# Five no-ops in place of two ahead of the first load on SyncE, in a rotary-embedding kernel

## The chip, the cores and the metric

One core of one Trainium2 chip. Times are device microseconds (us) of one execution, medians over several runs. An "interval" is the 95% interval of a ratio of times.

## The reference

```python
def reference(x, cos, sin, num_heads):            # x: 16 x 512 x 1024 f32, 16 heads of 64
    x = x.reshape(batch, seq, num_heads, head_dim)
    x1, x2 = x[..., :half_dim], x[..., half_dim:]
    cos, sin = cos[None, :, None, :], sin[None, :, None, :]     # 512 x 32 each
    return np.concatenate([x1 * cos - x2 * sin, x1 * sin + x2 * cos], axis=-1)
```

The kernel reads 33.5 MB and writes 33.5 MB; the two tables are 64 KB each.

## The kernel before

Eight tiles of 4 MB (128 partitions x 8 rows of 1024 floats). SyncE (SPq in the profile) issues all loads and stores of x and out on one queue; ScalarE (ACTq) issues the two tables on another. The start (comments put in here, cuts marked `# ...`):

```python
    nc.scalar.dma_start(out=sin_sb, in_=sin_v)        # L91, ScalarE's queue
    nc.scalar.dma_start(out=cos_sb, in_=cos_v)        # L92
    for _ in range(2):
        nc.sync.nop(hint="pause")                     # the two no-ops
    load(0, 0, FIRST[0])                              # tile 0, rows 0 to 2: 1.5 MB, 12 KB per partition
    for lo, hi in zip(FIRST, FIRST[1:]):
        load(0, lo, hi)                               # tile 0, rows 3 to 7: 20 KB per partition
    load(1)
    load(2)
    load_two(3)
    # ... identity matrix, then the tables are spread over 128 partitions by matmuls:
    nc.tensor.matmul(out=sin_t, lhsT=spread, rhs=sin_sb, start=True, stop=True)
    nc.tensor.matmul(out=cos_t, lhsT=spread, rhs=cos_sb, start=True, stop=True)
    # ... sns = (-sin, sin), in SBUF for GpSimd
```

Each tile: GpSimd multiplies by the sine rows (L175, `b`), DVE multiplies by the cosine (L151, into PSUM), multiplies one row of eight by the sine (L160) and adds most of the two (L199); PE and ScalarE add the rest. DVE starts when the cosine table is there, GpSimd when sine and the first x piece are. The kernel keeps five tiles in SBUF, so the later loads wait for stores:

```python
    def stores(t):
        if t == 4:
            store_two(3)
        elif t != 3:
            store(t)
        if t == 2:
            load(5)
            load_two(6)          # waits until the stores of tiles 1 and 2 have landed
```

## Time and profile before

| | before |
|---|---|
| time, median of 3 runs (spread) | 162.38 us (162.28 to 162.7) |
| span of the profiled run | 160.7 us |
| DVE, GpSimd busy | 136.3, 127.1 us |
| queue of x and out: share of 16 engines | 97.6% |
| sine, cosine landed | 7.2, 10.6 us |
| last store issued, landed | 148.23, 159.84 us |

A line of the timeline reads: start, duration, engine and line, operation, what it writes and reads, and in brackets how long the engine stood idle before and what ended that. From the timeline of the kernel before, the start of the two engines and the last store:

```profile
9.41 4.50 POOL L175 TENSOR_TENSOR b<-x,sns 128x2048 f32<-128x2048 f32 x1 [8.10 <-DVE sns L127]
...
12.18 1.23 DVE L151 TENSOR_TENSOR own_ps<-x,tab 128x1024 f32<-128x1024 f32 x1
...
148.23 0.33 SPq L83 DMA_DIRECT2D out_dram<-x  x1
```

GpSimd starts at 9.41 (released by the sine rows), DVE at 12.18 after the cosine table, and the last store is issued right after DVE's last sum; its 4 MB then take 11.6 us to land.

### The profile page before, as it was taken

What the parts mean: (1) busy time and instruction counts of PE and PEld (TensorE: products, weight loads), DVE (VectorE), ACT (ScalarE), POOL (GpSimd) and SP (SyncE); (2) the same over time, 40 slices, a digit from 0 to 9 for tenths busy, and PEclk for the clock granted to TensorE, in tenths of its full rate; (3) what the DMA queues carried; (4) which work ended last, traced back from release to release, by engine and by line L of the source; (5) the groups of instructions that cost most, each with busy time, mean ns of one, the idle gap of its engine ahead of it and who ended that gap; (6) DMA issues with size and microseconds to landing.
All of it is one profiled execution on the core that took longest, in us unless ns stands there. A gap on an engine that the chain in (4) does not pass through costs nothing.

```text
span 160.7 us, 433 instructions
## 1 busy us (share of the span) xinstructions
PE 57.2 (36%) x71; PEld 18.8 (12%) x71; DVE 136.3 (85%) x85; ACT 18.0 (11%) x25; POOL 127.1 (79%) x38
## 2 busy tenths in 40 slices
PE   3140825055503731191309250645047402922000
PEld 0110301021102210121003010211022101310000
DVE  1029999999999999999999999999999999998000
ACT  0000331003000301021100310031003010201000
POOL 1069999999999889988998899892999999960000
PEclk9999995558555765567555955585557655675555
DMA  5999999999999999999999999999999999999993
GB/s 168 411 431 458 408 473 424 392 449 465 392 449 449 408 392 506 408 392 498 410 400 465 441 400 441 465 392 432 473 400 416 489 400 416 473 408 408 392 506 147
DMA packets 2562, 67.25 MB, mean 419 GB/s; under 512 B 257, under 2 KB 385, under 8 KB 385
## 3 DMA queue, kind: packets, MB, share of 16 engines
q1 hardware_dynamic: 2400, 67.11, 97.6%
q10 hardware_dynamic: 160, 0.13, 0.2%
q14 instruction: 2, 0.01, 0.0%
HBM read 33.69 MB, written 33.55 MB: 418 GB/s over the span
## 4 chain that ended last, share of the span: by engine, by line
DVE 74%; issue 11%; DMA 6%; PE 1%; ACTq 0%; DVEq 0%
DVE x L199 34%; DVE pd L151 33%; DMA b<-in_cos_dram 6%; DVE pe_ps L151 5%; DVE own_ps L151 1%; PE tab L124 1%; ACTq L91 0%; DVE x L160 0%; DVE tab L129 0%; DVEq L199 0%
## 5 line engine op out<-in xcount | busy, mean ns | idle before, releaser
L175 POOL TENSOR_TENSOR b<-x,sns 128x2048 f32<-128x2048 f32 (+1 forms) x32 | 126.4, 3983 | 15.4 <-DVE sns L127 8.1
L199 DVE TENSOR_TENSOR x<-pd,b 128x2048 f32<-128x2048 f32 x24 | 54.9, 2288 | 0.9
L151 DVE TENSOR_TENSOR pd<-x,tab 128x2048 f32<-128x2048 f32 x24 | 55.0, 2292 | 0.2
L186 PE MATMUL own_ps<-x,ident 128*128 128x512 f32 x32 | 29.6, 1082 | 53.3 <-DVE x L160 48.3
L186 PE MATMUL pe_ps<-b,ident 128*128 128x512 f32 x32 | 25.1, 877 | 27.2 <-DVE pe_ps L151 27.2
L186 PEld LDWEIGHTS own_ps<-x,ident 128*128 128x128 f32 x32 | 9.4, 324 | 73.2 <-DVE x L160 59.3
L219 ACT COPY x<-own_ps 128x1024 f32<-128x1024 f32 x8 | 8.1, 1013 | 72.8 <-PE own_ps L186 72.8
L191 ACT COPY x<-pe_ps 128x512 f32<-128x512 f32 x16 | 9.4, 589 | 38.7 <-PE pe_ps L186 38.7
L186 PEld LDWEIGHTS pe_ps<-b,ident 128*128 128x128 f32 x32 | 8.2, 286 | 42.2 <-DVE pe_ps L151 33.9
L151 DVE TENSOR_TENSOR pe_ps<-x,tab 128x512 f32<-128x512 f32 x16 | 11.0, 687 | 0.0
L151 DVE TENSOR_TENSOR own_ps<-x,tab 128x1024 f32<-128x1024 f32 x8 | 9.8, 1224 | 0.0
L160 DVE TENSOR_TENSOR x<-x,tab 128x1024 f32<-128x1024 f32 x8 | 9.7, 1214 | 0.0
L126 DVE TENSOR_SCALAR sns<-pd 128x256 f32<-128x256 f32 x1 | 0.4, 425 | 7.0 <-PE pd L123 7.0
L219 ACT ACT_TABLE_LOAD x1 | 1.3, 1283 | 16.8 <-DVE x L160 16.8
L123 PE MATMUL pd<-b,spread 64*128 64x256 f32 x2 | 1.2, 696 | 4.7 <-DMA b<-in_sin_dram 4.7
L129 DVE COPY tab<-sns 128x64 f32<-128x64 f32 x1 | 0.2, 228 | 2.6 <-PE tab L124 2.6
L124 PE MATMUL tab<-b,spread 64*128 64x256 f32 x2 | 1.2, 708 | 2.1 <-DMA b<-in_cos_dram 2.1
L111 PE MATMUL own_ps<-zero 128*128 128x512 bf16 x2 | 1.0, 622 | 1.2 <-DVE zero L107 1.2
L123 PEld LDWEIGHTS pd<-b,spread 64*128 64x128 f32 x2 | 0.5, 306 | 5.6 <-issue 5.6
L107 DVE MEMSET zero<- 128x256 uint32 x1 | 0.3, 272 | 0.9 <-PEq L250 0.9
L124 PEld LDWEIGHTS tab<-b,spread 64*128 64x128 f32 x2 | 0.5, 310 | 2.9 <-DMA b<-in_cos_dram 2.9
L111 PE MATMUL pe_ps<-zero 128*128 128x512 bf16 x1 | 0.6, 634 | 0.0
(9 smaller groups left out, 1.8 us busy)
## 6 DMA issues: line engine op xcount, KB each, us to landing
out_dram<-x SPq DMA_DIRECT2D x6, 4096.0 KB, 21.4
x<-in_x_dram SPq DMA_DIRECT2D x2, 8192.0 KB, 39.5
x<-in_x_dram SPq DMA_DIRECT2D x3, 4096.0 KB, 27.2
out_dram<-x SPq DMA_DIRECT2D x1, 8192.0 KB, 32.6
x<-in_x_dram SPq DMA_DIRECT2D x1, 2560.0 KB, 12.4
x<-in_x_dram SPq DMA_DIRECT2D x1, 1536.0 KB, 6.6
b<-in_sin_dram ACTq DMA_DIRECT2D x1, 64.0 KB, 6.5
b<-in_cos_dram ACTq DMA_DIRECT2D x1, 64.0 KB, 9.3
```

The source lines that it names most:

```text
L107: nc.vector.memset(zero, 0.0)
L111: nc.tensor.matmul(out=ps, lhsT=zero[:, :P], rhs=zero, start=True, stop=True)
L123: nc.tensor.matmul(out=sin_t, lhsT=spread, rhs=sin_sb, start=True, stop=True)
L124: nc.tensor.matmul(out=cos_t, lhsT=spread, rhs=cos_sb, start=True, stop=True)
L126: nc.vector.tensor_scalar_mul(out=sns[:, :, 0, :], in0=sin_k, scalar1=-1.0)
L151: nc.vector.tensor_tensor(out=o, in0=i, in1=cb, op=ALU.mult)
L160: nc.vector.tensor_tensor(out=heads(r), in0=heads(r), in1=s, op=ALU.mult)
L175: nc.gpsimd.tensor_tensor(out=o, in0=i, in1=sb, op=ALU.mult)
L186: nc.tensor.matmul(out=ps, lhsT=ident, rhs=other, start=False, stop=True, skip_group_check=True)
L191: nc.scalar.copy(out=r, in_=pe_ps)
L199: nc.vector.tensor_tensor(out=r, in0=ps, in1=b, op=ALU.add)
L219: nc.scalar.copy(out=r0, in_=own_ps)
```

## The change

The intent: hold the first piece of x back a little longer, so that the tables, which start the compute, come in ahead of it.

```diff
-    for _ in range(2):
+    for _ in range(5):
         nc.sync.nop(hint="pause")
     load(0, 0, FIRST[0])
```

## The prediction

> **What bounds the kernel now.** I read the page from its second part (the span in 40 slices) and third part (queues) first, because the first part shows two engines near their limit and a share of a span does not say which of them ends last. Then the chain of waits, the DMA issues with their time to landing, and the timeline and the stretches at the two ends of the run.
>
> ```profile
> PE 57.2 (36%) x71; PEld 18.8 (12%) x71; DVE 136.3 (85%) x85; ACT 18.0 (11%) x25; POOL 127.1 (79%) x38
> DMA  5999999999999999999999999999999999999993
> q1 hardware_dynamic: 2400, 67.11, 97.6%
> q10 hardware_dynamic: 160, 0.13, 0.2%
> DVE 74%; issue 11%; DMA 6%; PE 1%; ACTq 0%; DVEq 0%
> ```
>
> The DMA row is 9 in every slice but the first and last. Queue q1 (all of x in and all of out, 67.11 MB) took 97.6% of the time of 16 engines, which is 0.976 x 160.7 = 156.8 us. DVE has 136.3 us. The chain of waits nevertheless follows DVE for 74% of the span, from the arrival of the cosine table on; a chain names one path and does not say that another, in transfers queued back to back, ends at the same time. So the question is whether DVE or the transfers set the last landing. The stretches at the two ends (columns: stretch, length, busy PE, PEld, DVE, ACT, POOL, clock, DMA share, GB/s; a packet counts in the stretch in which it starts, so shares over 1 occur):
>
> ```profile
> 0.00:1.80 1.80, 0.61 (x2) 0.28 (x3) 0.49 (x2) 0.00 (x0) 0.70 (x6) 1.00 0.00 0
> 12.00:52.00 40.00, 14.29 (x18) 5.07 (x19) 39.69 (x25) 5.46 (x7) 39.75 (x11) 0.69 1.01 431
> 52.00:82.00 30.00, 11.98 (x15) 3.55 (x14) 29.72 (x19) 4.18 (x6) 27.73 (x9) 0.61 1.00 433
> 82.00:111.00 29.00, 12.69 (x16) 4.39 (x16) 28.76 (x18) 3.59 (x5) 24.79 (x6) 0.62 1.00 433
> 111.00:148.00 37.00, 14.34 (x17) 4.56 (x16) 36.62 (x22) 4.78 (x7) 31.55 (x8) 0.59 1.02 438
> ```
>
> Nothing moves before 1.80 us, and from then the share is 1.00 to 1.02: both DMA and DVE are without a gap in the middle. The records of single packets decide it. They show 32 KB packets of 1.21 us each; the first starts at 1.83 us, the last ends at 159.51 us, and from 2.3 us to 148.6 us there are 16 in flight, but for gaps of nanoseconds. The store of tile 7 is issued at 148.23 us, right after DVE's last sum; the packets of the store before it end on the 16 engines between 148.6 and 149.8 us, and the new ones begin at 149.06 us. So most engines stand empty for up to 0.46 us there, but the slowest one goes on without a pause, and it is the one whose last packet ends at 159.5. Conclusion: the transfers bound the kernel from the first packet to the last, and DVE keeps up with about 0.8 us to spare (149.83 - 149.06).
>
> **What the Trainium skill says.** "PSUM — Partial Sum Buffer", section "Engine vs sequencer instructions": a no-op is a sequencer-only instruction, it runs on the sequencer and not on a datapath. The trace agrees: each of the two no-ops on SyncE took 13 ns, at 0.721 and 0.767 us (46 ns apart), with the first x piece issued at 0.828. "DMA: Bandwidth & Descriptors", section "Queues, rings and completion order": the transfers of SyncE and ScalarE have one ring each on the same 16 engines, and an engine alternates between rings packet by packet. The trace agrees: from 4.15 us each engine passes a 1 KB table packet (46 ns) about every 0.5 us, which is one 12 KB packet of x (0.46 us), later every 0.86 us beside 20 KB packets. Same page, section "Where 436 GB/s comes from": a ceiling of 435 GB/s; the trace has 431 to 438 in the middle, so there is no rate to be won. "Perfetto Trace Analysis", section on the HWDGE DMA instruction: the descriptor generator is shared by two issuing sequencers and held under a lock. The two issues below overlap, and the first table's took 0.54 us against 0.38 for the first x piece; that fits a lock but does not prove it.
>
> **The change part by part.** No other engine's instruction list moves; SyncE gets three more no-ops ahead of its first issue.
>
> ```profile
> 0.73 0.54 ACTq L91 DMA_DIRECT2D b<-in_sin_dram  x1
> 1.30 0.61 ACTq L92 DMA_DIRECT2D b<-in_cos_dram  x1
> x<-in_x_dram SPq DMA_DIRECT2D x1, 2560.0 KB, 12.4
> x<-in_x_dram SPq DMA_DIRECT2D x1, 1536.0 KB, 6.6
> b<-in_sin_dram ACTq DMA_DIRECT2D x1, 64.0 KB, 6.5
> b<-in_cos_dram ACTq DMA_DIRECT2D x1, 64.0 KB, 9.3
> ```
>
> Direct cost: 3 x 46 ns = 0.14 us. The first x issue goes from 0.83 to 0.97, and its end from 1.21 to 1.35. As the transfers have no slack from the first packet to the last, this is paid in full: +0.14 us.
>
> Order of the tables: now the x issue ends at 1.21 and the sine issue at 1.27. The x packets start at 1.83, and sine's first packet only at 4.15, after about five x packets per engine. With x ending at 1.35 the sine issue is over first, by 0.08 us. I expect the order to turn: sine's packets would start near 1.9 us. At the observed pace of one packet per 0.5 us, sine (4 packets and a semaphore write per engine) and then cosine (the same) need ten turns, 5 us. So cosine would land near 1.9 + 5 + 0.5 (from last packet to semaphore, as now: 10.16 to 10.62) = 7.4 us in place of 10.6, and sine near 4.9 in place of 7.2.
>
> What that gives the compute: GpSimd starts now at 9.41, released by the sine rows; then it would start when the first x piece is there, 0.83 + 6.6 = 7.4 now, some 7.6 then: 1.8 us earlier. DVE starts its first product at 12.18 now; then at about 9, 3 us earlier. But GpSimd's second product (row 3) needs the second x piece, which lands at 1.26 + 12.4 = 13.7 us, and it starts at 13.87 already now. So its second and third products stay where they are (13.87 + 2.3 + 4.5 = 20.7), and DVE's second pair sum waits for the third: at 20.7 in place of 21.84. What survives tile 0 is about 1.1 us of head start, not 3.
>
> What the head start gives the end: DVE's next check is the load of tiles 6 and 7.
>
> ```profile
> POOL b L175 <- DVE sns L127: 8.1, 1, 8.1
> POOL b L175 <- DMA x<-in_x_dram: 3.2, 1, 3.2
> 111.71 1.23 DVE L151 TENSOR_TENSOR own_ps<-x,tab 128x1024 f32<-128x1024 f32 x1
> 111.58 4.52 POOL L175 TENSOR_TENSOR b<-x,sns 128x2048 f32<-128x2048 f32 x1 [3.16 <-DMA x<-in_x_dram]
> ```
>
> That load lands at 111.44 us; GpSimd had waited 3.2 us for it, and DVE's first use of it starts at 111.71, only 0.27 us after the landing. Its landing is set by the queue, not by compute. A head start of 1.1 us is therefore spent waiting at 111.5; from there the 36.5 us of DVE work to 148.15 are the same. At most 0.2 us of earlier last store remains, and that store meets engines that are still busy until 149.8 at the slowest. Gain at the end: 0.
>
> Start of the stream: if sine holds the descriptor generator first, the x issue may wait for it a little. I chose +0.06 us for that: an even chance that some 0.12 us are lost, which is about half of the 0.16 us by which the sine issue outlasted the x issue now. The table packets themselves are only moved, not added (8 x 46 ns per engine before and after).
>
> Sum: +0.14 + 0.06 - 0 = +0.2 us. 162.38 + 0.2 = 162.6 us.
>
> **The rivals.**
> First, the chain of waits is right and the early cosine table pays: DVE is 74% of the chain, its start hangs on the cosine landing, so 1.1 to 3 us come off, 159.4 to 161.3 us. Against it: DMA packets are in flight without a gap to 148.6 us, and DVE would meet the same landing at 111.4. I hold this unlikely.
> Second, the order does not turn, because sine's lateness has another cause than the 0.06 us between the ends of the two issues. Then the tables land as now or 0.1 later, DVE starts 0.1 later, and the whole run shifts by 0.14: 162.5 us. The end can hardly tell this from my main case; the landings of the tables can.
> Third, the two issuers collide: ScalarE's two issues come one after the other and SyncE's x issue, now between them, waits for both. The x issue would then end near 1.9 instead of 1.35, the first packet at 2.5, and the end at 163.0 to 163.1. What speaks for it is that the second table's issue, at 0.61 us, took longer than the first; against it, SyncE's issues beside it took 0.42 us, no longer than usual.
> Fourth, a wait changes hands: GpSimd loses its lead over DVE (from 2.8 us at the start to about 1.4), so DVE waits for products in later tiles. GpSimd has 127.1 us of work against 136.3, about 1 us less per tile, so the lead grows again; and 0.8 us of tail slack covers a small loss. Worth 0 to 0.5 us.
>
> **Range and chances.** The three runs before span 162.28 to 162.7, so 0.2 us to either side is noise. Main case and second rival give 162.5 to 162.6, the third 163.1. Range: 162.1 (noise below, and no lock wait) to 163.1. Two per cent is 3.2 us, which no case but the extreme of the first rival comes near: faster 1%, slower 1%, within 98%.
>
> **What would show it right or wrong.** In the changed kernel's trace: five no-ops 46 ns apart and the x issue at about 0.97 us (step one); sine landing near 5 and cosine near 7.4 us instead of 7.2 and 10.6 (the order turned); first x packet near 1.97 to 2.1 us; DVE's first product near 9; GpSimd's second product still near 13.9 to 14.0; the landing of tiles 6 and 7 near 111.6, with DVE now waiting about 1 us ahead of its product there; last store issued near 148.2 to 148.4; DMA share still 1.00 in the middle. I am wrong on the bound if the last store comes over 1 us earlier and the time falls with it, wrong on the shift if the first x packet starts after 2.3 us, and wrong on the order if cosine still lands after 10 us.

## The result, and the profile after

162.78 us median of 6 runs (162.69 to 163.0) against 162.32 of 6 runs of before (162.24 to 162.7). A ratio is the mean time of one kernel's runs over that of the other's of the same rounds, so not quite the ratio of these medians: 1.0028, interval 1.0015 to 1.0041. That is 0.0028 x 162.3 = 0.45 us slower: within 2%, in the stated range, but twice the 0.2 us that was predicted.

From the page of the changed kernel, the same lines as of before:

```profile
PE 60.5 (38%) x71; PEld 19.2 (12%) x71; DVE 136.4 (85%) x85; ACT 18.6 (12%) x25; POOL 127.0 (79%) x38
DMA  5999999999999999999999999999999999999993
q1 hardware_dynamic: 2400, 67.11, 97.4%
q10 hardware_dynamic: 160, 0.13, 0.3%
DVE 41%; DMA 34%; issue 9%; POOL 7%; DVEq 0%; SPq 0%; POOLq 0%
```

Busy times and shares of the queues are as before; the chain of waits looks quite different. It was 74% DVE with the cosine load at its head; it now has 34% in transfers. The transfers did not become important by the change: they were limiting before as well, and the chain of before did not show it because DVE happened to arrive just after the load it needed.

The stretches (length, busy times, clock, DMA share, GB/s):

```profile
0.00:1.80 1.80, 0.61 (x2) 0.28 (x3) 0.49 (x2) 0.00 (x0) 0.70 (x6) 1.00 0.00 0
...
12.00:52.00 40.00, 16.63 (x19) 5.77 (x20) 39.41 (x25) 5.65 (x7) 38.42 (x11) 0.69 1.00 428
...
82.00:111.00 29.00, 14.18 (x16) 4.24 (x16) 28.55 (x18) 4.28 (x6) 23.75 (x6) 0.62 1.01 433
111.00:148.00 37.00, 13.71 (x16) 4.61 (x16) 35.84 (x21) 4.34 (x7) 31.54 (x8) 0.59 1.00 434
```

The DMA share in the middle is again 1.00. DVE has lost 36.62 - 35.84 = 0.78 us of busy time in the stretch from 111 to 148: a wait has come in. The issues of the tables and the transfers' times from issue to landing:

```profile
0.73 0.56 ACTq L91 DMA_DIRECT2D b<-in_sin_dram  x1
1.32 0.62 ACTq L92 DMA_DIRECT2D b<-in_cos_dram  x1
...
x<-in_x_dram SPq DMA_DIRECT2D x1, 1536.0 KB, 6.8
b<-in_sin_dram ACTq DMA_DIRECT2D x1, 64.0 KB, 2.4
b<-in_cos_dram ACTq DMA_DIRECT2D x1, 64.0 KB, 8.0
```

Sine lands after 2.4 us in place of 6.5, cosine after 8.0 in place of 9.3. The order has turned, and what that gave the compute, and where it was lost again, is in the timeline:

```profile
10.86 1.23 DVE L151 TENSOR_TENSOR own_ps<-x,tab 128x1024 f32<-128x1024 f32 x1
...
13.96 15.78 POOL L175 TENSOR_TENSOR b<-x,sns 128x1024 f32<-128x1024 f32 x4 [1.57 <-DMA x<-in_x_dram]
...
20.82 2.29 DVE L199 TENSOR_TENSOR x<-pd,b 128x2048 f32<-128x2048 f32 x1 [0.41 <-POOL b L175]
...
111.77 1.23 DVE L151 TENSOR_TENSOR own_ps<-x,tab 128x1024 f32<-128x1024 f32 x1 [0.98 <-DMA x<-in_x_dram]
111.81 4.52 POOL L175 TENSOR_TENSOR b<-x,sns 128x2048 f32<-128x2048 f32 x1 [3.73 <-DMA x<-in_x_dram]
...
148.29 0.33 SPq L83 DMA_DIRECT2D out_dram<-x  x1
```

DVE starts 1.3 us earlier. GpSimd's second product waits for the second x piece and starts at 13.96 (before: 13.87), so DVE's second pair sum comes at 20.82 (before: 21.84) after a wait of 0.41 us. The 1.02 us that remain are waited off at 111.77, where DVE needs tile 6; that load landed at 111.68 (before: 111.44). The last store is issued at 148.29, 0.06 us later than before.

The time comes from the other end. The records of single packets have the first x packet at 2.27 us in place of 1.83, and the slowest of the 16 engines has no gap from there to the end in which to make good. The profiled run is the fastest of its six (162.69 us, 0.31 over the profiled run of before), and its last packet ends 0.21 us later; the sum is drawn up below.

### The profile page after: what moved, and what is told of

The parts are those of the page before. It is cut to its first block, busy times and chain, and to the rows that moved or that the text cites. A ratio compares the mean times of both kernels' runs of the same rounds, so it can differ in the third digit from the quotient of the medians.

```text
span 160.9 us, 436 instructions
## 1 busy us (share of the span) xinstructions
PE 60.5 (38%) x71; PEld 19.2 (12%) x71; DVE 136.4 (85%) x85; ACT 18.6 (12%) x25; POOL 127.0 (79%) x38
## 4 chain that ended last, share of the span: by engine, by line
DVE 41%; DMA 34%; issue 9%; POOL 7%; DVEq 0%; SPq 0%; POOLq 0%
DMA x<-in_x_dram 22%; DVE x L199 21%; DVE pd L151 17%; DMA out_dram<-x 12%; POOL b L175 7%; DVE pe_ps L151 3%; DVE own_ps L151 0%; DVE x L160 0%; DVEq L199 0%; SPq L94 0%; POOLq L175 0%; SPq L80 0%; SPq L83 0%; DVEq L151 0%
## 5 line engine op out<-in xcount | busy, mean ns | idle before, releaser
L151 DVE TENSOR_TENSOR pd<-x,tab 128x2048 f32<-128x2048 f32 x24 | 55.0, 2292 | 0.2
L186 PE MATMUL own_ps<-x,ident 128*128 128x512 f32 x32 | 30.2, 1100 | 54.8 <-DVE x L160 49.9
L186 PE MATMUL pe_ps<-b,ident 128*128 128x512 f32 x32 | 28.0, 977 | 23.8 <-DVE pe_ps L151 23.8
L151 DVE TENSOR_TENSOR pe_ps<-x,tab 128x512 f32<-128x512 f32 x16 | 11.0, 685 | 0.0
L151 DVE TENSOR_TENSOR own_ps<-x,tab 128x1024 f32<-128x1024 f32 x8 | 9.8, 1224 | 1.0 <-DMA x<-in_x_dram 1.0
```

The lines of the kernel that those rows point to most:

```text
L151: nc.vector.tensor_tensor(out=o, in0=i, in1=cb, op=ALU.mult)
L186: nc.tensor.matmul(out=ps, lhsT=ident, rhs=other, start=False, stop=True, skip_group_check=True)
```

## The experiments

Three theories. **A** (the prediction's): the transfers bound the kernel from the first x packet to the last; what the change costs is the later start of that stream. **B**: each added no-op costs its share of the difference, 0.45/3 = 0.15 us, whatever the order. **C**: compute bounds the kernel, through the landing of the tables and the new waits of DVE and GpSimd. Ratios are always to the kernel before, of the same rounds on the same chip (medians of before: 162.50, 162.53 and 162.41 us in the three series). "Sine landed" and the like are from the traces.

### Fewer no-ops: none, three, four

```diff
-    for _ in range(2):
-        nc.sync.nop(hint="pause")
```

> No no-op on SyncE at all. Theory A (transfers bound; the end moves with the first x packet; the step of the change comes from sine passing x at the start): x issue at 0.72 us, first x packet 0.1 us earlier than before (1.73), order as before (x ahead of sine), time 0.1 us less than before, 162.2. Rival B (each no-op costs its share, 0.45/3 = 0.15 us): 0.3 us less than before, 162.0. Rival C (compute bound through the cosine landing): no change or slower if cosine lands later.

Measured without any no-op: 163.59 us, ratio 1.0063 (1.0051 to 1.0076), some 1.0 us slower. Theory A's time failed here, and so did B's, which wanted it faster. From this run's trace (two lines of the kernel are gone, so its L149 is L151 elsewhere):

```profile
b<-in_sin_dram ACTq DMA_DIRECT2D x1, 64.0 KB, 7.3
b<-in_cos_dram ACTq DMA_DIRECT2D x1, 64.0 KB, 11.0
...
13.80 1.23 DVE L149 TENSOR_TENSOR own_ps<-x,tab 128x1024 f32<-128x1024 f32 x1
...
149.81 0.33 SPq L83 DMA_DIRECT2D out_dram<-x  x1
```

The x stream did start 0.1 us earlier (1.74). But sine and cosine landed at 8.0 and 12.2, DVE started 1.6 us later (13.80 against 12.18), and the last store was issued 1.58 us later. The packet records show the 16 engines finishing the store before it between 148.7 and 149.9, and starting this one at 150.6: now every engine stood empty. So here compute ended last, as C said for the case that cosine lands later. The kernel before is balanced between two bounds: none to spare in the slowest transfers, under 1 us in compute. I had written down the small reserve (0.8 us at the last store) and not applied it to this run.

```diff
-    for _ in range(2):
+    for _ in range(3):      # and 4, in a run of its own
```

> Three no-ops. Theory A: the x issue trails the sine issue by 0.13 us and still ends 0.02 us before it, so I expect x still ahead of sine: first x packet near 1.87 us, sine landing near 7.2 us, time 0.04 us over before. If the order has turned already, first x packet near 2.2 and +0.4 us. Rival B (0.15 us for each no-op): +0.15 us whatever the order.

Measured with three: 162.60 us, ratio 1.0000 (0.9988 to 1.0012); order as before (sine landed at 7.2), first x packet at 1.88. As A expected; B's +0.15 us lies inside the interval of +-0.2 us, so this run alone does not exclude it.

> Four no-ops. Theory A: the x issue ends 0.02 us after the sine issue, so the order turns here: sine landing near 3.2 us, first x packet near 2.25, time +0.4 us over before, nearly all of the change. If not turned: +0.08. Rival B: +0.3 us.

> Four no-ops again. The first series had runs at 162.7 and at 163.1 to 163.3, and its profile had sine behind x (first sine packet at 3.87 us). If the order is a near tie here that falls either way, this profile may have sine at 2.1 us; if the order is fixed, sine is at 3.9 us again, and the time's two groups have another cause. Time +0.1 to +0.4 us over before.

Four, first series: 163.01 us, ratio 1.0026 (1.0012 to 1.0041), sine still behind x. Second series, the same kernel: 162.85 us, ratio 1.0024 (1.0011 to 1.0037), sine ahead of x. The issues of the profiled runs, first and second series:

```profile
b<-in_sin_dram ACTq DMA_DIRECT2D x1, 64.0 KB, 6.2
```

```profile
b<-in_sin_dram ACTq DMA_DIRECT2D x1, 64.0 KB, 2.9
```

The first x packet was at 1.91 in the first and at 2.49 in the second, the x issue at 0.90 in both. In the first the x issue ended 0.006 us before the sine issue, in the second 0.002 us. So at four no-ops the order is a near tie that falls either way, with one program; the two series ran on different chips, so whether it falls both ways on one chip is not shown. But the two profiled executions took 162.66 and 162.63 us, the fastest of their series, and their last packets ended 0.17 and 0.14 us later than before: in single runs the order does not tell the time, and what makes the two groups of times in the first series (162.7, and 162.9 to 163.3) stays open.

### The same no-ops, the order kept

Three no-ops ahead of ScalarE's table issues as well, so that x trails sine by 0.08 us, as it did before (0.10), and not by 0.20.

```diff
-    for _ in range(2):
+    for _ in range(5):
         nc.sync.nop(hint="pause")
...
+    for _ in range(3):
+        nc.scalar.nop(hint="pause")
     nc.scalar.dma_start(out=sin_sb, in_=sin_v)
```

> Five no-ops on SyncE and three ahead of the sine issue on ScalarE, so that x trails sine by about as little as before. Theory A: order as before (sine landing near 7.3 us, cosine near 10.7), first x packet at 1.94, time +0.11 us over before, a quarter of the change. Rival B (the no-ops on SyncE cost by themselves): +0.45 us as with the change. Rival C (DVE's or GpSimd's new waits in the middle are the cost): they vanish with the order, so +0.0 to +0.1; it is not told from A by the time, but by the landings.

> Repeat on one chip with the changed kernel, to tell 0.11 from 0.36 us. Theory A: +0.1 to +0.2 us over before. Rival B: the same as the changed kernel, +0.3 to +0.45.

> The changed kernel once more, so that the next three are compared with it on one chip: +0.4 to +0.5 us over before, first x packet near 2.27 us, sine ahead of x.

> The changed kernel a third time, beside the run above: +0.28 to +0.45 us over before as in the first two series.

| kernel | series 1 | series 2 | series 3 | mean |
|---|---|---|---|---|
| five no-ops (with the result above as series 1) | 1.0028 | 1.0017 | 1.0034 | 1.0026, or +0.43 us |
| five, and three ahead of the tables | 1.0013 | | 1.0008 | 1.0010, or +0.17 us |

From the first run with the order kept:

```profile
b<-in_sin_dram ACTq DMA_DIRECT2D x1, 64.0 KB, 6.5
b<-in_cos_dram ACTq DMA_DIRECT2D x1, 64.0 KB, 9.4
```

In both runs with the order kept, sine landed near 7.4 us and cosine near 10.8, and the first x packet was at 1.94 and 1.99 us, 0.10 and 0.16 later than before. The x issue came as late as in the changed kernel (0.93). So by the means about 0.17 us go with the later issue, and the remaining 0.26 us with sine being ahead of x; both sizes are rough. In the third series, on one chip and in the same rounds, the intervals of the two are 0.9993 to 1.0024 and 1.0018 to 1.0051: they hardly overlap. The second series had the changed kernel at 1.0017 (1.0005 to 1.0029), below its expectation of +0.4 to +0.5 us; one series doesn't fix the size to better than 0.2 us.

### More no-ops: a step or a slope

```diff
-    for _ in range(2):
+    for _ in range(8):      # and 24, in a run of its own
```

> Eight no-ops; the x issue at about 1.04 us, still inside the sine issue (to 1.29). Theory A with x held behind sine: the first x packet is set by sine's, so it stays near 2.3 us and the time stays within 0.15 us of the changed kernel's: a step, not a slope. If x is not held but merely starts a fixed 1.34 us after its issue: first packet 2.38, +0.11 us. Rival B (each no-op costs 0.15 us): +0.45 us over the changed kernel.

Eight: 162.87 us, ratio 1.0023 (1.0008 to 1.0038), the same as with five beside it (162.87 us, 1.0017). The x issue came 0.11 us later still (1.04), and the first x packet not at all (2.24): behind sine it waits for sine. (The median of the first 16 x packets did come later, 2.84 against 2.62 us with five beside it.) In the time this is a step, and B, which wanted 0.45 us more, falls for the stretch from five to eight.

> Twenty-four no-ops; at 0.037 us each the x issue comes at about 1.63 us, 0.8 later than before, and behind the cosine issue too. Theory A: first x packet at 2.6 to 3.0 us, both tables landed by 4 us, compute with slack, and the late start paid nearly in full: +0.5 to +1.0 us over before. Rival B (0.15 us for each no-op): +3.3 us. Rival C (compute bound, the early tables help): faster than the changed kernel.

Twenty-four: 164.13 us, ratio 1.0088 (1.0068 to 1.0108), +1.4 us; runs from 163.26 to 164.24. From this run's trace, landing times of the tables and a line of the waits (engine and tile waited with, what it waited for: total, times, longest):

```profile
b<-in_sin_dram ACTq DMA_DIRECT2D x1, 64.0 KB, 2.2
b<-in_cos_dram ACTq DMA_DIRECT2D x1, 64.0 KB, 3.2
...
DVE own_ps L151 <- DMA x<-in_x_dram: 4.3, 2, 2.3
```

Both tables were there by 4.5 us and DVE's first product started at 7.99, earlier than in any of the other kernels, and yet this kernel is the slowest: DVE waits 4.3 us for x. This speaks against C as plainly as the run without no-ops spoke for it on the other side. B's +3.3 us is excluded. But A's +0.5 to +1.0 is missed too. The first x packet at 2.88 us accounts for 1.05 us; the profiled run's last landing is 1.64 us later than before. In the packet records one part of the difference is slow 32 KB packets around 50 us, where the first loads end and the stores begin: 0.85 us per engine above 1.213 us each, against 0.18 before. That stretch is taken up below. Another part is the last store: after DVE's waits for x it is issued 1.46 us later than before (149.69), and the engines stand empty before it for 0.57 us on average, against 0.22 before.

### Extra work for DVE

Three memsets on DVE into a spare tile, in tile 1. By the issue of the next store they put DVE back by 1.8 us in the changed kernel (48.10 against 46.26 us) and by 2.0 in the kernel before (49.27 against 47.30).

```diff
+    spare = fixed.tile([P, 2 * BANK], BF16)
...
+        if t == 1:
+            for _ in range(3):
+                nc.vector.memset(spare, 0.0)
         r0 = rows(t, ROW_OWN)
```

> The changed kernel with three extra memsets on DVE in tile 1, some 1.6 us of DVE work in all. Theory A (transfers bound): DVE's 1.0 us wait for the load of tiles 6 and 7 disappears, the last store is issued some 0.6 us later, and the time stays within 0.2 us of the changed kernel's. Rival C (compute bound): 1.6 us slower than the changed kernel.

> The kernel before with the same three memsets. It has 0.27 us between the landing of tiles 6 and 7 and DVE's use of it, none to wait off, and some 0.8 us ahead of the slowest engine at the last store. Theory A: last store 1.6 us later, time 0.5 to 1.1 us over before, so clearly more than what the changed kernel loses by them. Rival C: 1.6 us slower than before. If DVE did not matter at all: no change.

In the changed kernel: 162.92 us, ratio 1.0022 (1.0010 to 1.0034), against 1.0017 without them beside it. By these ratios 1.8 us of DVE work cost 0.1 us, give or take 0.2. In the kernel before: 164.01 us, ratio 1.0091 (1.0076 to 1.0105), +1.5 us, more than the 0.5 to 1.1 expected: the last store came 1.97 us later (150.20) and not 1.6, and the reserve that this leaves, 1.97 - 1.48, is 0.5 us and not 0.8. The run without no-ops gives 0.6 (1.58 - 1.02). From the timeline of the changed kernel with the memsets:

```profile
112.52 1.22 DVE L151 TENSOR_TENSOR own_ps<-x,tab 128x1024 f32<-128x1024 f32 x1
...
149.03 0.33 SPq L83 DMA_DIRECT2D out_dram<-x  x1
```

The wait before tile 6 is gone and the last store is 0.7 us later, but the engines were still busy with the store before it until 149.0 to 150.0 us, and took up the new one from 149.86: most stood empty for a while, the slowest hardly. From the stretches of the kernel before with the memsets:

```profile
149.00:150.00 1.00, 0.00 (x0) 0.00 (x0) 1.00 (x1) 0.00 (x0) 0.00 (x0) 0.50 0.08 33
150.00:151.00 1.00, 0.00 (x0) 0.00 (x0) 0.13 (x1) 0.00 (x0) 0.00 (x0) 0.50 0.00 0
```

Here hardly a packet starts between 149 and 151 us: the engines have run dry and wait for DVE. The same work is nearly free in one kernel and costs three quarters of its length in the other. That is what the change has really done: it moved about 1 us of reserve to compute and took some 0.4 us from the transfers, whose slowest engine had none.

No kernel of the series beats the kernel before; two and three no-ops are equal within the interval, and none, four, five, eight and 24 are slower; a single one was not run.

## Why the prediction was right or wrong

**The bound: right,** shown by the runs with extra DVE work and with 24 no-ops. One restriction, seen in the run without no-ops: the reserve of compute is so small, 0.5 to 0.6 us where the prediction read 0.8, that 1.6 us of later cosine turns the bound over.

**The direct cost: +0.14 predicted, 0.11 measured.** The x issue moved from 0.828 to 0.935 us. The no-ops came 46, 40, 37 and 35 ns apart; I had taken the one spacing that the trace before showed for all.

**The order: right that it turns, wrong in how.** Sine's packets did not alternate with x; all of them started between 2.07 and 2.81 us, 58 of the 64 before half of the engines had their first x packet, so sine landed at 3.18 us, not 4.9. Cosine did not follow at one packet in 0.5 us: its first packet started at 5.7 us, after 97 of the 128 packets of the first x piece, so it landed at 9.30 and not 7.4. The pace that I read from the trace before holds once a queue is in turn with another, not for the wait until it is.

**The compute's head start: right** where it mattered (1.02 us left after tile 0, 1.1 predicted; wait of 0.98 before tile 6; last store at 148.29), though DVE started at 10.86 and not near 9.

**The start of the stream: the term that was mis-sized.** "+0.06 us for that: an even chance that some 0.12 us are lost" was far too little. The first x packet came 1.01 us after its issue before and 1.34 us after it now, so being behind sine cost 0.33 us. (With four no-ops and sine ahead it came 1.59 us after its issue, so this cost is no fixed one.) With the issue itself, the first x packet is 0.44 us later, where the sum had 0.20. By the prediction's own sign (wrong on the shift if the first x packet starts after 2.3 us) the three profiled runs of the changed kernel stand at the edge: 2.27, 2.26 and 2.35.

**Why this is not exactly the measured 0.43 us** is seen only in the packet records. In the three profiled runs of the changed kernel (in parentheses the kernel before) the median of the first 16 x packets started at 2.46, 2.62, 2.74 us (1.98), so the stream was later by 0.47 to 0.76. The packets of the first two x pieces then took 10.52, 10.31, 10.23 us per engine (10.67), which gives 0.15 to 0.44 back. And packets around 50 us took 0.26, 0.32, 0.37 us per engine above 1.213 us each (0.18), 0.08 to 0.19 more. The last term I had not thought of. It was 0.04 to 0.18 in all kernels with the order of before and 0.24 to 0.85 in all with the order turned, so it goes with the turned order and the later start that comes with it; why, none of the runs tells.

These three add up to 0.40 to 0.51 us, but they are not the whole account: averaged over the 16 engines, the last packets ended only 0.09, 0.26 and 0.30 us later, and the slowest engine's 0.21, 0.41 and 0.46. Two more terms give time back. Sine's packets, now ahead of x, no longer interrupt the stream, 0.1 to 0.2 us per engine: "only moved, not added" held for the packets, not for the time after the first x packet. And before the last store the engines stood empty for 0.07 to 0.13 us on average in place of 0.22, so the shift was not paid in full. Slow packets elsewhere, mostly from 100 to 110 us, add 0.02 to 0.12. That the first profile's last packet came 0.21 us later, just the predicted 0.2, is therefore luck: a start that cost double, less returns that were not foreseen.

**The rivals of the prediction:** the first (early cosine pays) fell; the second (order does not turn) fell for five no-ops, and holds for three; the third (collision of the issuers) was right that x is held up behind sine, wrong in that it would wait for both table issues (x issue ending near 1.9, first packet at 2.5): it ended at 1.32, with the first packet at 2.27. The fourth was seen once, at 0.41 us in tile 0, at no cost to the end.

## What to carry to other kernels

When a queue of transfers is busy without a gap from first to last packet, look at when its first packet starts; a later start is paid for there, if not always in full, and a chain of waits that runs through a compute engine does not show it. A pause that lets a small transfer ahead of a large one moves time from one bound to another, so it pays only up to where the two bounds meet, and that place is found by a sweep rather than by going further in the direction that helped. To learn which bound has the reserve, add a known piece of work to one engine: here it cost next to nothing where there was reserve and three quarters of its length where there was little.

## What the Trainium skill lacked or had wrong

- "DMA: Bandwidth & Descriptors", section "Queues, rings and completion order", says that an engine takes turns between queues packet by packet. The traces agree once both queues are in turn (a table packet every 0.5 us beside 12 KB packets). It lacks the wait before that: sine, whose issue ended at 1.27 us, had its first packet at 4.15, some five x packets later; in the changed kernel cosine, whose issue ended at 1.94, had its first at 5.7.
- The same page, section "Latency and other measured facts", gives about 0.6 us to the first byte for a transfer issued by these engines. The first x packet before started 0.62 us after the end of its issue, in agreement if that is where it is counted from; behind the other issuer's transfer it was 0.95 us (1.32 to 2.27). The page has no figure for that.
- "Advanced Engine Details and Errata", section "Clock Domains", tells what a no-op with a cycle count waits; no page gives the cost of one without. Here: 13 ns recorded, 35 to 46 ns from one to the next on SyncE.
- No page says that two transfers whose issues end within 0.01 us of each other can reach the engines in either order: with four no-ops the first sine packet was at 3.87 us in one profile and at 2.07 in the other, on another chip.
- No page has the slow packets where loads give way to stores: 32 KB packets of 1.21 us took up to 1.6 us there before, and up to 2.0 us in the kernel with 24 no-ops.
